# A two-block network on one core: gates ahead of gMLP's mixing, another order of routing, and an extra expert slot of 64 places

## The chip, the core and the metric

The kernel runs on one core of one Trainium2 chip. The metric is the device time of one execution in microseconds (us), with all inputs and outputs in device memory. A core has TensorE (PE, matrix products into PSUM), VectorE (DVE), ScalarE (ACT) and GpSimd (POOL) on the on-chip memory, SyncE (SP), which here issues most transfers, and 16 transfer engines that all queues share. POOL issues the indirect transfers (gather and scatter of rows) and those that add to what lies in memory.

## What is computed

512 positions of width 1024 pass through two residual blocks, all in float32. The reference, cut to what matters here:

```python
x = first_block(x, ...)          # SSD and RWKV mixers, then a gated feed-forward net
h = rms_norm(x, g1) * (1 + sc1) + sh1
ys = gmlp(h), gla(h), sparse_attention(h)                 # (512, 512) each
gate = sigmoid(h @ w_gates + b)                           # (512, 3, 1024)
merged = sum over n of gate[:, n] * (ys[n] @ w_branch[n]) # 24 tiles of 128 columns
x = x + gt1 * (merged @ w_out)
h2 = rms_norm(x, g2) * (1 + sc2) + sh2
grp = argmax(softmax(h2 @ w_group + b_group))             # 1 of 4 groups of 4 experts
e1, e2 = top 2 of the router's logits in that group
x = x + gt2 * sum over e in (e1, e2) of weight_e * (silu(h2 @ Wg[e]) * (h2 @ Wu[e])) @ Wd[e]
```

gMLP mixes positions inside chunks of 128: `y = u * (w_s @ layer_norm(v) + b_s)`, a lower triangular `w_s` for each of four groups of columns. An expert has 1024 x 256 weights for Wg and Wu and 256 x 1024 for Wd.

## The kernel before

**Products.** A float32 product is made of three faster ones: `split` (L186, L187) and the weight loads (L155, L156 and, for the experts, L1307, L1308) make of a tile a rounded part `hi` on ACT and the remainder `lo` on DVE; then hi x hi, lo x hi and hi x lo are added in PSUM (L170 to L172). Weights come in pieces of 512 KB, 128 x 1024, by SP. The trace shows such a split product with PE rows of three lines; a product of plain f32 operands stands as two rows.

**The start.** Seventeen products of zeros (L278) run until the first operands are there. SP loads `vec` (L136), then the eight blocks of x (L284); ACT loads the first raw weights (L283).

**Branches and gates.** `ev_v` (L1066 to L1074) evaluates gMLP's `v` with gelu on ACT and normalises it on DVE. The mixing products (L1078) need all of `v`, then L1079 and L1080 make `u`, and `merge(0, u)` (L986) splits it into `yh` and `yl`. `merge(n)` runs over eight column tiles d: a gate product (24 instructions, `gemm` with `win2`, tanh on ACT at L991), then the branch product (12, `wbr`), then one or two operations on DVE (L993 to L996). Up to the routing a scheduler sets each engine's order, by costs and due times; it mixes the sparse attention (L1092 to L1105) with the merge of gMLP. Two tiles `th` hold gates.

**Routing.** The second half of `w_out` and the routing have their order written out. For each block of 128 positions tb: eight products (`product`, L1312), with the block before turned (`turned`, transposes L1321), its logits (`logits` L1325, `added` L1328 to L1331) in between; then `x2half` (L1279 to L1281) adds the residual and squares on ACT; `inverse` (L1333 and the Newton steps L228 to L233) makes 1/rms; `scaled` (L1336) and `rows_out` (L1340 to L1344) write h2's rows to the DRAM buffer `d_h2`. For blocks 0 and 1 `d_h2` is filled with the shift sh2 beforehand and POOL adds the rows to it (L1341); for blocks 2 and 3 DVE adds the shift (L1343) and SP writes (L1344). Then DVE finds group, experts and each row's place in its expert's list (L1365 to L1408), and POOL gathers the first 128 rows (L1467).

**Experts.** 17 slots of 128 places: 16 experts, and a slot 16 for the first expert whose list is longer than 128; its number is read from a register, and a branch covers further overflow. A slot e: rows are gathered (L1467), transposed (L1473) and split; four up pieces (L1484 to L1486, 24 instructions); silu on ACT (L1488), the product on DVE (L1489); transposes (L1493); two down pieces (L1503 to L1506, of which L1506 is plain f32 and has no split); DVE scales (L1507), and POOL scatters the rows to `out`, adding (L1508). The loop (L1541) computes up(e+1) between the parts of down(e). Five of the six pieces of a slot are split on ACT and DVE. SP issues the weight loads in the order of `todo`, as slots of a ring of some 22 tiles come free; only the first ten are asked for ahead of the first gather (`hold`). `further` (L1425) works out on DVE, in five steps, which experts overflow; `extra` (L1443) looks up the rows of the overflow in one piece at e = 11. In the order rows below, numbers behind names such as `gv_8091` are buffers.

## Time and profile before

| quantity | value |
|---|---|
| three runs | 1485.41, 1489.78, 1494.95 us; median 1489.78 us |
| profiled execution | 1490.69 us; span 1488.9 us, granted clock 0.979 |
| PE busy | 1423.3 us, 96% of the span |
| DVE busy | 1028.4 us, 69% |
| ACT busy | 642.4 us, 43% |
| POOL busy | 94.9 us, 6% |
| from HBM / to HBM | 208.06 / 27.03 MB |
| expert stage | PE resumes at 1299.43 us, last scatter issued at 1478.26 us |

The span runs from the first to the last instruction; the profiled execution has 1.8 us around it. Busy shares are means over stages with different limits. Where PE is busy almost all the time, what counts is which wait interrupts it, at which clock it runs, and what lies behind its last product.

### The profile page before, as it was taken

The numbers are of one execution on the slowest core, as the hardware profiler recorded it, in microseconds if no ns is written. First come the engines' busy times: TensorE is split into PE (matmuls) and PEld (weight loads), VectorE is DVE, ScalarE is ACT, GpSimd is POOL, SyncE is SP. The second block draws the span as 40 slices with busy tenths as digits, with TensorE's granted clock in tenths as the row PEclk, the third lists the DMA queues.
The fourth block names the chain that finished last, engine by engine and source line by source line (L and its number), as shares of the span: only waits on it lengthen the run. The fifth ranks groups of instructions, "written<-read, shape, count | busy, mean of one in ns | idle before, by whom it ended". The sixth has DMA issues, their size and how long they took to land. (4 is left out here: it accounts for less than half of the span.)

```text
span 1488.9 us, 22888 instructions
## 1 busy us (share of the span) xinstructions
PE 1423.3 (96%) x8863; PEld 1107.0 (74%) x8863; DVE 1028.4 (69%) x1948; ACT 642.4 (43%) x1045; POOL 94.9 (6%) x114
## 2 busy tenths in 40 slices
PE   9999998999999999999999989999899999599996
PEld 5777877677777787778777777777678887377774
DVE  6788977578777767544749867654544344789995
ACT  6554374234443443223443324463622333266663
POOL 0121000000000000000001000000000000123321
PEclk9999998999999999999999999999999999799999
DMA  5347234143556535553424211222044234499992
GB/s 215 134 154 251 85 112 133 66 142 124 167 177 212 183 115 188 172 170 114 146 99 140 92 57 50 64 95 80 23 167 138 92 127 165 142 391 362 331 342 58
DMA packets 78885, 226.16 MB, mean 152 GB/s; under 512 B 19571, under 2 KB 20211, under 8 KB 78771
## 3 DMA queue, kind: packets, MB, share of 16 engines
q1 hardware_dynamic: 68626, 201.79, 39.0%
q0 software_dynamic: 8992, 19.71, 4.8%
q10 hardware_dynamic: 1152, 3.15, 0.5%
q8 instruction: 71, 1.16, 0.3%
q14 instruction: 44, 0.35, 0.1%
HBM read 208.06 MB, written 27.03 MB: 158 GB/s over the span
## 5 line engine op out<-in xcount | busy, mean ns | idle before, releaser
L155 ACT ACTIVATE hi<-raw 128x1024 fp32r<-128x1024 f32 (+1 forms) x181 | 181.1, 1001 | 395.6 <-PE g L171 255.2
L156 DVE TENSOR_TENSOR lo<-raw,hi 128x1024 fp32r<-128x1024 f32 (+1 forms) x181 | 208.1, 1150 | 203.5 <-ACT hi L155 202.9
L172 PE MATMUL g<-bh,lo 128*128 128x512 f32 x376 | 152.4, 405 | 2.6 <-DVE lo L156 2.4
L170 PE MATMUL g<-bh,hi 128*128 128x512 f32 x376 | 152.1, 405 | 0.0
L171 PE MATMUL g<-bl,hi 128*128 128x512 f32 x376 | 150.3, 400 | 0.0
L170 PE MATMUL g<-hh,hi 128*128 128x512 f32 x336 | 133.1, 396 | 0.0
L172 PE MATMUL g<-hh,lo 128*128 128x512 f32 x336 | 132.7, 395 | 0.2 <-DVE lo L156 0.2
L171 PE MATMUL g<-hl,hi 128*128 128x512 f32 x336 | 132.6, 395 | 0.0
L172 PEld LDWEIGHTS g<-bh,lo 128*128 128x128 f32 x376 | 71.5, 190 | 22.6 <-DVE lo L156 4.1
L170 PEld LDWEIGHTS g<-bh,hi 128*128 128x128 f32 x376 | 71.7, 191 | 19.3 <-issue 2.4
L171 PEld LDWEIGHTS g<-bl,hi 128*128 128x128 f32 x376 | 71.4, 190 | 16.2 <-issue 0.2
L170 PE MATMUL g<-xh,hi 128*128 128x512 f32 x192 | 76.8, 400 | 0.0
L170 PEld LDWEIGHTS g<-hh,hi 128*128 128x128 f32 x336 | 63.3, 188 | 17.7 <-ACT hi L155 2.5
L172 PE MATMUL g<-xh,lo 128*128 128x512 f32 x192 | 76.4, 398 | 0.0
L171 PE MATMUL g<-xl,hi 128*128 128x512 f32 x192 | 76.2, 397 | 0.0
L172 PEld LDWEIGHTS g<-hh,lo 128*128 128x128 f32 x336 | 63.3, 188 | 15.5 <-DVE lo L156 0.6
L171 PEld LDWEIGHTS g<-hl,hi 128*128 128x128 f32 x336 | 63.3, 189 | 14.6
L885 DVE SCALAR_TENSOR_TENSOR acc<-raw,ca,acc 128x1024 f32<-128x1024 f32 x42 | 53.8, 1282 | 28.7 <-DMA raw<-in_wmod 28.4
L914 DVE SCALAR_TENSOR_TENSOR c<-g,vec,c 128x511 f32<-128x511 f32 x88 | 65.6, 745 | 1.1
L777 PE MATMUL g<-hi,fh 128*128 128x512 f32 x136 | 53.9, 396 | 0.0
L779 PE MATMUL g<-lo,fh 128*128 128x512 f32 x136 | 53.7, 395 | 0.0
L778 PE MATMUL g<-hi,fl 128*128 128x512 f32 x136 | 53.7, 395 | 0.0
(705 smaller groups left out, 3200.7 us busy)
## 6 DMA issues: line engine op xcount, KB each, us to landing
raw<-in_wexp SPq DMA_DIRECT2D x89, 512.0 KB, 13.2
raw<-in_win SPq DMA_DIRECT2D x72, 512.0 KB, 3.5
raw<-in_wmod SPq DMA_DIRECT2D x48, 512.0 KB, 4.1
raw<-in_wup SPq DMA_DIRECT2D x44, 512.0 KB, 4.3
raw<-in_wdn SPq DMA_DIRECT2D x22, 512.0 KB, 3.9
raw<-in_wout SPq DMA_DIRECT2D x16, 512.0 KB, 4.8
ws<-in_wexp SPq DMA_DIRECT2D x13, 512.0 KB, 14.3
raw<-in_wA SPq DMA_DIRECT2D x12, 512.0 KB, 3.9
```

The costliest lines, as they stand in the source:

```text
L155: S.activation(hi[:,:f],raw[:,:f],AF.Copy)
L156: V.tensor_tensor(lo[:,:f],raw[:,:f],hi.bitcast(F32)[:,:f],op=OP.subtract)
L170: PE.matmul(ps,hi[:,sl],xh[k],start=(k==0),stop=False)
L171: PE.matmul(ps,hi[:,sl],xl[k],start=False,stop=False)
L172: PE.matmul(ps,lo[:,sl],xh[k],start=False,stop=(k==n-1))
L777: PE.matmul(ps,xh[k][:,sl],w[kk][0],start=(k==0),stop=False)
L778: PE.matmul(ps,xl[k][:,sl],w[kk][0],start=False,stop=False)
L779: PE.matmul(ps,xh[k][:,sl],w[kk][1],start=False,stop=(k==2*n-1))
L885: else: V.scalar_tensor_tensor(acc,raw,ca[:,k:k+1],acc,op0=OP.mult,op1=OP.add)
L914: for k in (1,2): V.scalar_tensor_tensor(c[:,k:],ps[:,:512-k],Vc(f'fw{2-k}',i),c[:,k:],op0=OP.mult,op1=OP.add)
```

## The change

Six things are done at once.

- Start: `vec` is loaded on ACT's queue, x's first block is asked for first on SP, and two of the seventeen zero products go.
- Gates: `gate(n, d)` makes one gate ahead of its use; three are made before gMLP's mixing, and `merge` keeps three ahead. Four tiles `th` instead of two.
- Routing: all four blocks' rows are added by POOL to a `d_h2` that is filled with the shift for all 512 rows, so the tile of the shift goes. `rows_out(tb-1)` and `added(tb-1)` stand before the last three products of block tb; the last block is scaled before its inverse and multiplied by it on ACT.
- Clock: 13 products whose result nobody reads (`keep_going`) stand between the places' products and the first slot, and five before the last down product.
- Look-up: `extra` becomes `extra_steps`, four pieces at e = 7 to 10; `further` starts one slot earlier, and a further overflow test is added (a list of more than 192 rows, or a second overflow, takes the branch).
- Extra slot: it holds 64 places and runs between experts 14 and 15. Its products are plain f32 on unsplit weights, each in two halves of 64 columns of the array (`up64`, `down64`), so none of its six pieces is split; expert 15 comes last.

Places where the order moves, engine by engine.

PE around the last of gMLP's mixing (`m<-wst`, L1078 before, L1086 now; `g<-bh`, `g<-bl` are gate products, `m<-kn` the attention's first product). Before:

```order
L170 MATMUL g<-bh,hi 128x512
L171 MATMUL g<-bl,hi 128x512
L172 MATMUL g<-bh,lo 128x512
L1078 MATMUL m<-wst,gv_8127 128x128 x4
L1078 MATMUL m<-wst,gv_8145 128x128 x4
L1092 MATMUL m<-kn_7624,yq_7068 128x128
L170 MATMUL g<-yh,hi 128x512
```

Now, from the fourth mixing product on; behind the dots stand gate products alone, then the other twelve mixing products:

```order
L1086 MATMUL m<-wst,gv_8107 128x128
L172 MATMUL g<-bh,lo 128x512
L170 MATMUL g<-bh,hi 128x512
L171 MATMUL g<-bl,hi 128x512
...
L172 MATMUL g<-bh,lo 128x512
L1086 MATMUL m<-wst,gv_8125 128x128
L1086 MATMUL m<-wst,gv_8143 128x128
...
L1086 MATMUL m<-wst,gv_8143 128x128
L1100 MATMUL m<-kn_7622,yq_7066 128x128
L170 MATMUL g<-yh,hi 128x512
```

Of the 72 instructions of the first three gates, 71 stand ahead of the last twelve mixing products; before, 32 gate instructions stood ahead of the last eight.

DVE from block 3's residual to the first operation of the routing (`L1365` before, `L1372` now). Before:

```order
L1280 TENSOR_TENSOR x1t<-x1t,g_11690 128x512
L1343 SCALAR_TENSOR_TENSOR h_11643<-h_11643,nv,modr 128x1024
L1333 TENSOR_SCALAR nv<-ssq 128x1
...
L1336 TENSOR_TENSOR h_11705<-x1t,modr 128x1024
L1329 TENSOR_REDUCE l_11723<-m 128x20
L1330 TENSOR_TENSOR lg<-lg,l_11723 128x20
L1331 SCALAR_TENSOR_TENSOR lg<-lg,nv,rbias 128x20
L1343 SCALAR_TENSOR_TENSOR h_11705<-h_11705,nv,modr 128x1024
L1365 TENSOR_REDUCE mx_11738<-lg 128x20
```

Now:

```order
L1348 SCALAR_TENSOR_TENSOR h_11675<-x1t,nv,modr 128x1024
L1337 TENSOR_REDUCE l_11680<-m 128x20
L1338 TENSOR_TENSOR lg<-lg,l_11680 128x20
L1339 SCALAR_TENSOR_TENSOR lg<-lg,nv,rbias 128x20
L1287 TENSOR_TENSOR g_11687<-g,modr 128x512
L1288 TENSOR_TENSOR x1t<-x1t,g_11687 128x512
L1344 TENSOR_TENSOR h_11692<-x1t,modr 128x1024
L1341 TENSOR_SCALAR nv<-ssq 128x1
...
L1337 TENSOR_REDUCE l_11720<-m 128x20
L1339 SCALAR_TENSOR_TENSOR lg<-lg,nv,rbias 128x20
L1372 TENSOR_REDUCE mx_11733<-lg 128x20
```

Block 2's rows (L1348) stand ahead of block 3's residual instead of behind it; block 3's scaling stands ahead of its inverse, and no pass over its rows is left before L1372.

PE in the extra slot, which before was a slot like the others. Now (`L1533` transposes, `L1540` up, `L1553` down, `L1512` and `L1492` transposes of the neighbours):

```order
L1533 MATMUL m<-cst,xg 128x64 x8
L1522 MATMUL g<-hi,ah 128x512
...
L1525 MATMUL g<-raw,af 128x512
L1540 MATMUL g<-raw,xf 64x256 x8
L1512 MATMUL m<-cst,a 128x128 x2
L1540 MATMUL g<-raw,xf 64x256 x8
L1492 MATMUL m<-cst,xg 128x128 x8
...
L1547 MATMUL m<-cst,a_13445 128x64 x2
...
L1553 MATMUL g<-raw,af_13494 64x512 x4
```

Sixteen up and four down products stand in place of 24 and eight, and expert 15's products follow between and behind them.

The diff, changed lines only:

```diff
@@ -133,7 +133,7 @@
-    vec=cp.tile([128,A['vec'].shape[1]],F32,name='vec'); nc.sync.dma_start(vec,A['vec'])
+    vec=cp.tile([128,A['vec'].shape[1]],F32,name='vec'); nc.scalar.dma_start(vec,A['vec'])
@@ -275,13 +275,14 @@
-        for _ in range(17): PE.matmul(zp,zb[:,:128],zb,start=True,stop=True)
+        for _ in range(15): PE.matmul(zp,zb[:,:128],zb,start=True,stop=True)
...
+        nc.sync.dma_start(xt[0],A['xT'][0])
...
-        for k in range(8): nc.sync.dma_start(xt[k],A['xT'][k])
+        for k in range(1,8): nc.sync.dma_start(xt[k],A['xT'][k])
@@ -966,7 +967,8 @@
-    mpool=pool('mp',bufs=2,stack=ph2)
+    GA=3
+    mpool=pool('mp',bufs=GA+1,stack=ph2)
@@ -981,14 +983,19 @@
+    gates={}
+    def gate(n,d):
+        ps=gemm(w2b(23+8*n+d),hh,hl)
+        gates[n,d]=th=mpool.tile([128,512],F32,name='th',tag='th'); S.activation(th,ps,AF.Tanh,bias=bgh[:,8*n+d:8*n+d+1],scale=0.5)
...
-            ps=gemm(w2b(23+8*n+d),hh,hl)
-            th=mpool.tile([128,512],F32,name='th',tag='th'); S.activation(th,ps,AF.Tanh,bias=bgh[:,8*n+d:8*n+d+1],scale=0.5)
+            for d2 in range(d,min(8,d+GA)):
+                if (n,d2) not in gates: gate(n,d2)
+            th=gates[n,d]
@@ -1035,7 +1042,7 @@
-    with tc.issue_after(oh_.ins): nc.sync.dma_start(d_h2[0:256,:],bass.AP(tensor=d_mod.tensor,offset=d_mod.offset+3072,ap=[[0,256],[1,1024]]))
+    with tc.issue_after(oh_.ins): nc.sync.dma_start(d_h2,bass.AP(tensor=d_mod.tensor,offset=d_mod.offset+3072,ap=[[0,512],[1,1024]]))
@@ -1073,6 +1080,7 @@
+    for d in range(GA): gate(0,d)
@@ -1228,7 +1236,7 @@
-    slots=[(rawm,'raw')]*NR+[(wr,'raw')]*4+[('pe',f'modr{i}') for i in (0,2,1)]+[(res_pool,f'res{i}') for i in range(4)]+[('AS',0),('AS',1),('AS',2),('AS',3),('pe2','rx0')]
+    slots=[(rawm,'raw')]*NR+[(wr,'raw')]*4+[('pe',f'modr{i}') for i in (1,0,2)]+[(res_pool,f'res{i}') for i in range(4)]+[('AS',0),('AS',1),('AS',2),('AS',3),('pe2','rx0')]
@@ -1240,7 +1248,7 @@
-    for e in range(1,16): todo+=wx(e,range(4))+wx(e-1,(4,5))
+    for e in range(1,15): todo+=wx(e,range(4))+wx(e-1,(4,5))
@@ -1257,10 +1265,10 @@
-    for i in range(4):
+    for i in (0,2,3):
...
-    gt1r,sh2r,a2r,gt2r=modr
+    gt1r,a2r,gt2r=modr
@@ -1309,9 +1317,9 @@
-    def product(tb,ps,p):
+    def product(tb,ps,p,kks=(0,1)):
...
-        for kk in range(2):
+        for kk in kks:
@@ -1336,26 +1344,25 @@
-        if tb<2:
+        if tb<3:
...
-            G.dma_start(d_h2[tb*128:tb*128+128,:],h,accum_op=OP.add)
...
-            h=blk[tb]['h']; V.scalar_tensor_tensor(h,h,v,sh2r,op0=OP.mult,op1=OP.add)
-            nc.sync.dma_start(d_h2[tb*128:tb*128+128,:],h)
+            h=blk[tb]['h']; S.activation(h,h,AF.Copy,scale=v)
+        G.dma_start(d_h2[tb*128:tb*128+128,:],h,accum_op=OP.add)
...
-        product(tb,ps,3)
-        if tb: added(tb-1)
+        product(tb,ps,3,(0,))
+        if tb: rows_out(tb-1); added(tb-1)
+        product(tb,ps,3,(1,))
...
-        if tb: rows_out(tb-1)
+        if tb==3: scaled(tb)
...
-        if tb>=2: scaled(tb)
-    turned(3); logits(3); added(3); rows_out(3)
+    turned(3); logits(3); rows_out(3); added(3)
@@ -1403,6 +1410,10 @@
+    def keep_going(n):
+        w=pt()
+        for _ in range(n): PE.matmul(w,trib[:,:128],Ak[:,0:4,:].rearrange('p i s -> p (i s)'),start=True,stop=True)
+    keep_going(13)
@@ -1439,32 +1450,40 @@
-        V.tensor_copy(ei[:,0:7],EQ[:,0,0:7]); V.tensor_copy(ei[:,7:8],pos[:,47:48])
-    def extra(j,ps,s):
+        mc=pe_.tile([128,1],F32,name='mc'); V.tensor_reduce(mc,cnt,axis=AX,op=OP.max)
+        V.scalar_tensor_tensor(mc,mc,192.5,pos[:,47:48],op0=OP.is_gt,op1=OP.add)
+        V.tensor_copy(ei[:,0:7],EQ[:,0,0:7]); V.tensor_copy(ei[:,7:8],mc)
+    def extra_steps(j,ps,s,upper=False):
...
-        V.tensor_scalar(cc,cc,EQ[:,1,j:j+1],None,op0=OP.subtract)
+        V.tensor_scalar(cc,cc,EQ[:,1,j:j+1],64.0 if upper else 0.0,op0=OP.subtract,op1=OP.subtract)
+        yield
...
+        yield
...
-        return onehot(cc),lambda tb:tb_[:,tb,:],ps,s
+        yield
+        O=onehot(cc)
+        if upper: V.memset(O[:,:,64:],0.0)
+        yield O,lambda tb:tb_[:,tb,:],ps,s
+    def extra(*a,**k): return list(extra_steps(*a,**k))[-1]
...
-    for s_ in range(1,17): pieces+=[(s_,p) for p in range(4)]+[(s_-1,4),(s_-1,5)]
-    pieces[-6:]=[(16,0),(16,1),(15,4),(15,5),(16,2),(16,3),(16,4),(16,5)]
+    for s_ in range(1,15): pieces+=[(s_,p) for p in range(4)]+[(s_-1,4),(s_-1,5)]
+    pieces+=[(16,p) for p in range(4)]+[(14,4),(14,5),(15,0),(15,1),(16,4),(16,5)]+[(15,p) for p in range(2,6)]
...
-            s_,p=pieces[len(done)]; done.append(wnext(p==5 or (s_<NW and p<4)))
+            s_,p=pieces[len(done)]; done.append(wnext(p==5 or s_==16 or (s_<NW and p<4)))
...
-    def gather(ix):
+    def gather(ix,n=128):
...
-        G.indirect_dma_start(out=xg,out_offset=None,in_=d_h2,in_offset=bass.IndirectOffsetOnAxis(ap=ix,axis=0),bounds_check=511,oob_is_err=False)
+        G.indirect_dma_start(out=xg[:n],out_offset=None,in_=d_h2,in_offset=bass.IndirectOffsetOnAxis(ap=ix,axis=0),bounds_check=511,oob_is_err=False)
@@ -1507,6 +1526,34 @@
+    def rows64(xg):
+        xf=pe2.tile([128,8,64],F32,name='xf',tag='xgl',bufs=1)
+        for hf in range(2):
+            ps=pt((128,4,64))
+            for kk in range(4): PE.transpose(ps[:,kk,:],xg[:64,(4*hf+kk)*128:(4*hf+kk)*128+128],ident[:64,:64])
+            S.activation(xf[:,4*hf:4*hf+4,:],ps,AF.Copy)
+        return xf
+    h64=lambda e: slice(64*e,64*e+64)
+    def up64(ps,xf,p,raw):
+        for kk in range(2):
+            k=2*p+kk
+            for e in range(2): PE.matmul(ps[h64(e),:256],xf[:,k],raw[:,kk*512+256*e:kk*512+256*e+256],start=(k==0),stop=(k==7))
+    def end64(ps,wcol):
+        u=sq_pool.tile([64,256],F32,name='u64',tag='sq',bufs=3); V.tensor_scalar(u,ps[64:,:256],wcol[:64],None,op0=OP.mult)
+        a=sq_pool.tile([64,256],F32,name='a64',tag='sq',bufs=3); S.activation(a,ps[:64,:256],AF.Silu)
+        V.tensor_tensor(a,a,u,op=OP.mult); return a
+    def act64(a):
+        pT=pt((128,2,64))
+        for f in range(2): PE.transpose(pT[:,f,:],a[:,f*128:f*128+128],ident[:64,:64])
+        af=pe2.tile([128,2,64],F32,name='af64',tag='afx',bufs=1); S.activation(af,pT,AF.Copy)
+        return af
+    def down64(af,raws,ix):
+        y=pe2.tile([128,1024],F32,name='ye',tag='ye',bufs=3); ps=psum()
+        for f in range(2):
+            for e in range(2): PE.matmul(ps[h64(e)],af[:,f],raws[f][:,512*e:512*e+512],start=(f==0),stop=(f==1))
+        for e in range(2): V.tensor_tensor(y[:64,512*e:512*e+512],ps[h64(e)],gt2r[h64(e),512*e:512*e+512],op=OP.mult)
+        G.indirect_dma_start(out=out,out_offset=bass.IndirectOffsetOnAxis(ap=ix,axis=0),in_=y[:64],in_offset=None,
+                             bounds_check=511,oob_is_err=False,compute_op=OP.add)
@@ -1538,36 +1585,49 @@
-    for e in range(17):
+    for e in range(14):
...
-        if e<13: xgs.append(gather(idx[:,e+4:e+5]))
-        if e==3: fur=further()
-        if 3<=e<8: next(fur,None)
-        if e==11: xps=pm.tile([128,17,8],F32,name='m',tag='m'); O=extra(0,xps,16)
-        if e==8:
+        if e<11: xgs.append(gather(idx[:,e+4:e+5]))
+        else: xgs.append([lambda:gather(idx[:64,16:17],64),lambda:gather(idx[:,15:16]),lambda:None][e-11]())
+        if e==2: fur=further()
+        if 2<=e<7: next(fur,None)
+        if e==7: xst=extra_steps(0,None,16)
+        if 7<=e<10: next(xst)
+        if e==10: xps=pm.tile([128,17,8],F32,name='m',tag='m'); o_=next(xst); O=(*o_[:2],xps,16)
+        if e==7:
...
-            w0=[(A['wexp'][bass.ds(e0,1),p].rearrange('o p f -> (o p) f'),p==5) for p in range(6)]
-            todo+=w0[:2]+wx(15,(4,5))+w0[2:]
-        if e<16: ps=psum(); up_piece(ps,xin,0,piece(e+1,0))
+            w0=[(A['wexp'][bass.ds(e0,1),p].rearrange('o p f -> (o p) f'),True) for p in range(6)]
+            todo+=w0[:4]+wx(14,(4,5))+wx(15,(0,1))+w0[4:]+wx(15,range(2,6))
+        ps=psum(); up_piece(ps,xin,0,piece(e+1,0))
...
-        if e<16:
-            for p in range(1,4):
-                if e==15 and p==2: down(aa,piece(e,4),piece(e,5),idx[:,e:e+1])
-                up_piece(ps,xin,p,piece(e+1,p))
-            a=up_end(ps,wcl[:,e+1:e+2])
+        for p in range(1,4): up_piece(ps,xin,p,piece(e+1,p))
+        a=up_end(ps,wcl[:,e+1:e+2])
...
-        if e<15: xin=rows_in(xgs[e+2],e+2)
-        if e!=15: down(aa,piece(e,4),piece(e,5),idx[:,e:e+1])
+        xin=rows_in(xgs[e+2],e+2) if e<13 else rows64(xgs[15])
+        down(aa,piece(e,4),piece(e,5),idx[:,e:e+1])
...
+    ps=psum()
+    for p in range(2): up64(ps,xin,p,piece(16,p))
+    aa=act_in(a)
+    for p in range(2,4): up64(ps,xin,p,piece(16,p))
+    a=end64(ps,wcl[:,16:17])
+    xin=rows_in(xgs[16],15)
+    down(aa,piece(14,4),piece(14,5),idx[:,14:15])
+    ps=psum(); up_piece(ps,xin,0,piece(15,0)); af=act64(a)
+    up_piece(ps,xin,1,piece(15,1))
+    down64(af,(piece(16,4),piece(16,5)),idx[:64,16:17])
+    for p in range(2,4): up_piece(ps,xin,p,piece(15,p))
+    a=up_end(ps,wcl[:,15:16]); keep_going(5)
+    down(act_in(a),piece(15,4),piece(15,5),idx[:,15:16])
...
-    nx=nc.values_load(ei[0:1,7:8],min_val=0,max_val=7)
+    nx=nc.values_load(ei[0:1,7:8],min_val=0,max_val=8)
...
-        for j in range(1,7): placed(*extra(j,xps,j))
-        infos(xps,1,7,wc2,ix2)
-        for j in range(1,7):
+        for j in range(7): placed(*extra(j,xps,j,upper=j==0))
+        infos(xps,0,7,wc2,ix2)
+        for j in range(7):
```

## Rows read from the trace of the kernel before

**Rows 1.** Waits of PE over the whole span: total us, times, longest us.

```profile
PE m L1473 <- DMA xg<-d_h,idx: 5.8, 1, 5.8
PE g L172 <- DVE lo L156: 2.6, 4, 1.8
PE g L1486 <- DVE ws L1308: 1.9, 1, 1.9
```

**Rows 2.** Windows: from:to, length; busy us of each engine, granted clock, DMA share, GB/s.

```profile
888.00:898.00 10.00, 5.95 (x23) 5.00 (x24) 8.63 (x18) 4.04 (x7) 0.00 (x0) 0.68 0.19 72
1300.00:1340.00 40.00, 38.86 (x177) 29.41 (x176) 34.62 (x56) 27.42 (x40) 9.39 (x7) 0.94 1.02 384
1340.00:1380.00 40.00, 40.00 (x180) 29.99 (x178) 39.47 (x56) 27.35 (x42) 15.06 (x8) 1.00 1.01 360
1380.00:1420.00 40.00, 40.00 (x180) 30.19 (x179) 36.86 (x50) 27.25 (x41) 11.40 (x9) 1.00 0.99 341
1420.00:1460.00 40.00, 38.14 (x171) 28.93 (x170) 36.56 (x54) 23.76 (x37) 8.97 (x5) 0.96 0.88 304
```

**Rows 3.** Timeline of the start: start us, duration, engine, line, operation, idle before.

```profile
0.76 0.40 SPq L136 DMA_DIRECT2D vec<-in_vec  x1
6.43 0.72 ACT L189 ACTIVATE xh<-x,vec 128x512 fp32r<-128x512 f32 x1 [2.29 <-DMA x<-in_xT]
```

**Rows 4.** Timeline, PE at the last gMLP mixing.

```profile
890.45 1.16 PE L1078 MATMUL m<-wst,gv 128*128 128x128 f32 x8 [2.77 <-DVE gv L1074]
892.74 2.08 PE L1078 MATMUL m<-wst,gv 128*128 128x128 f32 x8 [1.14 <-DVE gv L1074]
895.71 0.80 PE L170 MATMUL g<-yh,hi 128*128 128x512 f32 x1 [0.46 <-ACT yh L186]
```

**Rows 5.** Timeline, DVE between the last product and the first routing operation.

```profile
1286.12 1.28 DVE L1343 SCALAR_TENSOR_TENSOR h<-h,nv,modr 128x1024 f32<-128x1024 f32 x1
1287.32 0.23 DVE L1365 TENSOR_REDUCE mx<-lg 128x20 f32<-128x80 f32 x1
```

**Rows 6.** Timeline, POOL's first row gather and PE's resumption.

```profile
1294.96 1.19 POOL L1467 DMA_INDIRECT xg<-d_h,idx  x1 [17.45 <-DVE idx L1408]
1299.43 1.94 PE L1473 MATMUL m<-cst,xg 128*128 128x128 f32 x8 [5.84 <-DMA xg<-d_h,idx]
```

**Rows 7.** One line, the two accumulating row writes.

```profile
DMA to landing us min/median/max: 5.0/5.1/5.2
```

**Rows 8.** Timeline, PE: f32 products of 64 columns, then of the whole array.

```profile
215.65 0.39 PE L600 MATMUL g<-ring,Sin 128*64 128x128 f32 x4
215.87 0.39 PE L598 MATMUL g<-ring 128*64 128x128 f32 x4
...
934.28 1.05 PE L1104 MATMUL m<-pT,dv 128*128 128x128 f32 x8
935.09 0.48 PE L171 MATMUL g<-yl,hi 128*128 128x512 f32 x1
```

**Rows 9.** Timeline, down products of three expert slots, and DVE's look-up between.

```profile
1417.37 0.79 PE L1503 MATMUL g<-ws,ah 128*128 128x512 f32 x1
...
1421.50 0.23 DVE L1445 TENSOR_SCALAR eq<-cst,EQ 128x16 f32<-128x16 f32 x1
...
1424.35 0.68 DVE L1411 TENSOR_TENSOR O<-cst,xcc 128x512 bf16<-128x512 f32 x1
...
1440.90 0.80 PE L1503 MATMUL g<-hi,ah 128*128 128x512 f32 x1
...
1450.71 0.79 PE L1503 MATMUL g<-hi,ah 128*128 128x512 f32 x1
```

**Rows 10.** One line, the loads of the expert weights.

```profile
DMA to landing us min/median/max: 3.6/13.2/18.0
```

**Rows 11.** Chain that ended last: start us, us, what.

```profile
1471.65 5.84 DMA out<-ye,idx
```

**Rows 12.** One line, the scatters of the expert rows.

```profile
DMA to landing us min/median/max: 3.9/9.0/10.6
```

## The prediction, on record before the change was timed

> **What bounds the kernel now.** I read the waits of TensorE (PE) first, because PE is busy for 96% of the span: a change can only gain what PE idles, what it does at half clock, what it need not do, and what lies behind its last product. The waits [rows 1] name two places that the diff touches, 5.8 us for the first gathered rows and 1.9 us in an expert slot, and in the timeline gMLP's mixing [rows 4]. Then the windows [rows 2], to be read in two columns. The granted clock, against 1.00, tells where PE runs at the lower of its two levels (1.2 instead of 2.4 GHz): 0.68 at 888 to 898, 0.94 at 1300 to 1340, 0.96 at 1420 to 1460. The DMA share tells how full the transfer engines are during the experts: 1.02, 1.01, 0.99, then 0.88. PE is busy for all 40 us of two of these windows, yet the transfers are full too, so what PE gains there may not be kept. Last the chain that ended last [rows 11]: behind the last product the end is a row of scatters, each waiting for the one before.
>
> **Start.** SP's load of `vec` takes 0.40 us of issue ahead of x, and ACT's first split waits for x [rows 3]. On ACT's queue it delays the raw blocks instead. Bounds: 0 and -0.4; I take **-0.3**, since x is the one named as the releaser.
>
> **Gates ahead of the mixing.** PE idles 2.77, 1.14 and 0.46 us here [rows 4], 4.37 in all. The clock of 0.68 means 64% of 10 us at half speed, 6.4 us; 1.6 of these are the last two gaps, so some 4.8 us of work cost 2.4 too much. The ceiling is 6.8 us. In the new order 71 gate products stand ahead of the last mixing products where there were 32; 39 at 0.222 us (180 in the 40 us of a full window [rows 2]) are 8.7 us, more than gap and slow clock together. PE does no less work; it pays because those 8.7 us go missing later, where they cover nothing that the rows show waiting. The price is on DVE, busy 8.63 of these 10 us [rows 2]: it makes two more low halves before the split of `u`, and ACT's `yh` still follows the mixing. For those waits I keep 0.8, taken from the 0.46 and 1.14 that PE waits today; if the split comes late by the whole 2.77 the gain is 3.5. **-6.0**, between -3.5 and -6.8. The later gates only trade places: every product keeps its weights, its conversions and its load on SP, which are asked for in the new order.
>
> **Routing.** DVE's two passes by line 1343, of which [rows 5] show the second, 1.28 us, are on the path: the first, alike, stands ahead of the last inverse, the second delays routing's first operation to 1287.32. The change puts the first one before the block's last products end and leaves the second to ACT, behind which nothing waits but POOL's write. So 2 x 1.28 go, and the third block's logits move ahead of the last three products, 0.7 us, of which I count 0.5; the last logits still pass ACT and PE and may come when DVE has long been free, for which I take 0.7 back (no row shows when). **-2.4**, between -1.3 (one pass) and -3.1. The new danger is the write: accumulating writes took 5.0 to 5.2 us to land [rows 7]. If POOL issues the last no earlier than DVE finished it before, 1286.12 + 1.28, it lands at 1292.6; the gather, now at 1294.96 [rows 6] less 2.4, starts at 1292.6 as well. So it costs nothing until it is late, then one for one. The prefilled rows add 1 MB long before, in stretches where the transfers have room (share 0.19 at 888 to 898).
>
> **Clock at the first slot.** PE waits 5.84 us for the rows and resumes at 1299.43 [rows 6]. A clock of 0.94 over 40 us is 4.8 us at half speed, 2.4 us lost. Thirteen 512-column products at half clock (twice 0.222 us) are 5.8 us and just fit into the wait. They buy the clock, but then the first pieces' conversions on ACT and DVE decide: **-1.6**, between 0 and -2.4.
>
> **Look-up in four steps.** From the down product of one slot to the next takes 9.81 us (1440.90 to 1450.71), and the two slots with the look-up take 23.53 [rows 9]: 3.91 too much, of which 1.9 is PE's wait for DVE [rows 1] and the rest clock (0.96). On DVE it runs from 1421.50 to 1425.03, 3.5 us with one short break [rows 9]. In four steps, four slots to one slot earlier, it falls into 1382 to 1412. At 1380 to 1420 DVE is busy 36.86 of 40 us, so 0.77 per slot is free for 0.9 per slot. **-3.4**, between -2 and -3.9. DVE at 39.47 of 40 one window earlier says how thin that cover is.
>
> **Extra slot of 64 places.** Today a slot: 9.81 us. In f32 a product stands as two records. With 64-column outputs the next four records follow after 0.22 us; with the whole array eight take 0.81 [rows 8], so 0.055 against 0.101 each: the two column halves run together. The new slot's 16 products of 256 columns are 32 records of twice the length, 3.5 us; its 4 of 512 columns 8 records of four times, 1.7; ten smaller transposes at 0.055 add 0.6: 5.8. **-4.0**; one after the other it would be 6.5 + 3.2 + 0.6 = 10.3, +0.5, the other bound. The Trainium skill (TensorEngine Tiling (Array Packing), "Key Properties") says that a change of tiling mode drains TensorE, which speaks against a slot that goes in and out of it. As an estimate, the 0.17 us by which a group of [rows 8] outlasts the next one's start, at six changes, is 1.0, and the sum would be -3.0; no row here shows such a drain.
>
> **What the transfers take back.** Clock, look-up and slot give 9.0 us after the weights have begun to flow (routing's 2.4 moves the flow too). The transfers have 12% of 40 us, 4.8, to spare in one window, none before [rows 2]; gather and scatter of 64 rows instead of 128 save 0.5 MB, 1.4 us at 341 to 360 GB/s. So between 0 and 2.8 us of the gain must wait for weights that are asked for 13.2 us ahead [rows 10]: **+1.3**, the middle. Expert 15's pieces, now last, are where it shows.
>
> **Tail.** The last scatter was the extra slot's, which holds the fewest rows; I take the shortest for it, 3.9 us [rows 12]. It becomes expert 15's, which took 5.84 [rows 11]: **+2.0**. The five fillers ahead of the last transposes cost 0.1 at most beside a wait that is there anyway.
>
> **Sum.** -0.3 - 6.0 - 2.4 - 1.6 - 3.4 - 4.0 + 1.3 + 2.0 = -14.4. The profiled execution took 1490.69 us (span 1488.9, 1.8 around it), 0.9 above the median: 1476.3 for such an execution, **1475** for the median.
>
> **Rivals.**
> - *Nothing taken back*: no late weights (1.3), no leftover at gates, look-up (0.8, 0.5) and clock (0.8): 1472. For it: DVE and transfers have some slack wherever the gain falls. Against: three of four windows at 0.99 or more.
> - *The halves do not run together*, so that the slot does not do what it is cut for: +4.5, 1480. Against: 0.055 per record; for: those records move 128 columns, these 256 and 512.
> - *The transfers keep their old pace*: the whole 9.0 is lost instead of 1.3, 1483. For it: shares of 0.99 to 1.02; against: 0.88, and PE, not the queue, set the two long slots.
> - *Slower than before*: in the merges the branch products now follow gates of which three are ahead, and DVE's low halves come late. PE waited for low halves 4 times, 2.6 us [rows 1]. If each of the 24 branch products waited such 0.65 us, it would be 15.6: 1491; at the longest, 1.8, 43 us: 1518. It decides from 0.6 us per product for slower at all, from 1.25 for slower by over 1%. Against: only four such waits in all the gemms now.
>
> **Numbers.** Forecast 0.50 (its own range 1469 to 1481), nothing taken back 0.15, halves 0.15, transfers 0.14, slower 0.04, the rest 0.02. A run of this kernel tells 1% from no change: 14.9 us, 1474.9. The forecast lies on that line, so half of it counts as faster: 0.25 + 0.15 + the rest of 0.02, 0.42. Within 1%: 0.55. Slower by over 1%: 0.03, the long form of the last rival. The range 1467 to 1484 takes in the first three rivals and the bounds of the gates and the slot.
>
> **What would show it.** Right: no PE gap over 0.5 us and a clock near 1.00 at 885 to 900; routing's first reduction about 2.4 us sooner against the last product; no half clock behind the first gather; no wait for DVE in the look-up's slots; the extra slot at 5 to 7 us between its neighbours; the last scatter near 5.8. Wrong: PE waits for conversions whose weights have just landed, in expert 15 above all; a gather that waits for POOL's last accumulating write; new waits for low halves between gates and branch products; a mixing that waits as long as before, only later.

## The result, and the profile after

The changed kernel takes **1480.63 us** (median of 13 runs, 1475.24 to 1487.36) against 1489.78 us for the kernel before (13 runs beside them): ratio 0.9936, 95% interval 0.9919 to 0.9952, so 9.2 us or 0.6% faster. The forecast was 14.4 us. The profiled execution took 1484.45 us, span 1482.7 us, granted clock 0.979.

To see where the time went I cut both traces at the same events, each the start of an instruction, and compare the stretches between them (us; "again" is a second profile of the change, its text unchanged, span 1482.2). The first stretch begins with the span:

| from the event before to | before | after | again |
|---|---|---|---|
| second block's `hn`, first product | 718.31 | 720.92 | 718.37 |
| first product of the linear attention's own gate | 266.30 | 259.39 | 259.01 |
| its first score product | 47.35 | 46.72 | 46.72 |
| its last | 33.11 | 35.19 | 35.07 |
| routing's first transpose | 184.51 | 184.40 | 185.03 |
| routing's first reduction (`mx`) | 37.74 | 35.12 | 35.11 |
| PE's first transpose of gathered rows | 12.11 | 12.17 | 12.23 |
| third slot's transposes (so: two slots) | 17.85 | 18.22 | 18.22 |
| last down product | 159.13 | 152.44 | 153.48 |
| end | 12.49 | 18.12 | 18.96 |

Gates give 7.5 us (rows two and three; 7.9 in the second profile), but 2.1 and 2.0 of it go again in row four, and PE's clock went with them:

```profile
1031.96:1065.07 33.11, 27.23 (x917) 20.14 (x916) 27.01 (x70) 19.71 (x56) 0.00 (x0) 0.95 0.05 14
```

```profile
1027.03:1062.22 35.19, 28.99 (x917) 21.68 (x916) 28.02 (x71) 20.70 (x57) 0.00 (x0) 0.86 0.09 32
```

These are row four's windows (columns as in [rows 2]), before and after: the same 917 products, the granted clock 0.95 and 0.86. Routing gives 2.6 us. PE reaches its last product 6.7 us sooner after the third slot began (5.6 in the second profile), but 5.6 to 6.5 us are lost behind that product. From the third slot to the end it is 171.6 us before, 170.6 and 172.4 after. The 2.6 us in the first stretch is no work of the change: from 100 to 120 us the granted clock was 0.83 in this profile, 0.91 in the second and 1.00 before, and a run below whose start is that of the kernel before (four pieces ahead) takes 721.40 us here.

Windows of the changed kernel, columns as in [rows 2]:

```profile
886.00:896.00 10.00, 10.00 (x49) 8.27 (x48) 9.86 (x30) 2.82 (x4) 0.00 (x0) 1.00 0.23 79
896.00:906.00 10.00, 9.28 (x54) 7.95 (x53) 5.59 (x12) 4.59 (x8) 0.00 (x0) 1.00 0.23 79
1290.00:1330.00 40.00, 36.42 (x164) 26.64 (x163) 33.26 (x58) 26.62 (x38) 9.89 (x9) 0.94 0.96 358
1330.00:1370.00 40.00, 40.00 (x181) 30.34 (x180) 39.69 (x59) 26.62 (x41) 13.43 (x8) 1.00 1.02 370
1370.00:1410.00 40.00, 40.00 (x185) 30.17 (x184) 39.42 (x54) 26.59 (x41) 13.60 (x8) 1.00 0.97 336
1410.00:1450.00 40.00, 40.00 (x201) 28.67 (x199) 31.93 (x45) 23.40 (x39) 10.14 (x6) 1.00 0.97 334
1430.00:1450.00 20.00, 20.00 (x107) 13.43 (x106) 13.20 (x18) 9.80 (x19) 3.16 (x2) 1.00 0.93 331
```

The clock at the mixing is 1.00 where it was 0.68, and the 40 us from 1410 run at 1.00 without a gap where those from 1420 had 0.96 and 38.14 busy [rows 2]. Only 1290 to 1330 still shows 0.94.

The timeline of the changed kernel, PE at the mixing and the extra slot, ACT before it, then POOL and DVE at the end:

```profile
899.91 2.84 PE L1086 MATMUL m<-wst,gv 128*128 128x128 f32 x24
903.70 0.50 PE L170 MATMUL g<-yh,hi 128*128 128x512 f32 x1 [0.72 <-ACT yh L186]
...
1443.29 1.95 PE L1540 MATMUL g<-raw,xf 128*64 128x256 f32 x16
1445.17 0.44 PE L1512 MATMUL m<-cst,a 128*128 128x128 f32 x2
1445.54 1.95 PE L1540 MATMUL g<-raw,xf 128*64 128x256 f32 x16
1454.81 1.94 PE L1553 MATMUL g<-raw,af 128*64 128x512 f32 x8
...
1443.89 1.06 ACT L1315 ACTIVATE ws<-raw 128x1024 fp32r<-128x1024 f32 x1 [3.40 <-DMA raw<-in_wexp]
...
1458.57 1.54 POOL L1527 DMA_INDIRECT out<-ye,idx  x1 [6.46 <-DVE ws L1316]
1465.01 1.43 POOL L1555 DMA_INDIRECT out<-ye,idx  x1 [4.90 <-DVE ye L1526]
1465.20 0.69 DVE L1526 TENSOR_TENSOR ye<-g,modr 128x512 f32<-128x512 f32 x1 [0.87 <-PE g L1525]
1470.19 1.55 POOL L1527 DMA_INDIRECT out<-ye,idx  x1 [3.74 <-DMA out<-ye,idx]
```

Read the last three together. Expert 15's result is complete at 1465.20 + 0.69 = 1465.89, but its scatter is issued at 1470.19, 4.3 us late: all scatters add to `out`, each waits for the one before, and the extra slot's went off at 1465.01. Before, the last result was complete at 1477.73 and its scatter issued at 1478.26, 0.5 us later. The releaser at 1465.01 reads `DVE ye`, yet that scatter too started just behind its predecessor, which landed at 1464.26 in the chain of the changed kernel (start us, us, what):

```profile
1410.92 9.29 DMA out<-ye,idx
...
1422.02 9.15 DMA out<-ye,idx
1431.97 9.40 DMA out<-ye,idx
1442.16 7.64 DMA out<-ye,idx
1450.55 7.24 DMA out<-ye,idx
1458.57 5.69 DMA out<-ye,idx
1465.01 4.42 DMA out<-ye,idx
```

Here is the bound that [rows 11] showed only the end of: from 1410.92 on the end is set by scatters. Most start 0.8 us behind the landing of the one before; they are some 9 us long, and shorter towards the end. PE is busy for every one of the 40 us to 1450 and does not stand in this chain.

### The profile page after: what moved, and what is told of

The parts are those of the page before. It is cut to its first block, busy times and chain, and to the rows that moved or that the text cites. A ratio compares the mean times of both kernels' runs of the same rounds, so it can differ in the third digit from the quotient of the medians.

```text
span 1482.7 us, 22891 instructions
## 1 busy us (share of the span) xinstructions
PE 1422.2 (96%) x8883; PEld 1103.1 (74%) x8885; DVE 1019.0 (69%) x1941; ACT 635.6 (43%) x1038; POOL 97.4 (7%) x116
## 4 chain that ended last, share of the span: by engine, by line
PE 77%; DVE 10%; DMA 5%; issue 3%; ACT 3%; SPq 0%; POOL 0%; POOLq 0%; ACTq 0%; DVEq 0%
PE g L172 14%; PE g L170 13%; PE g L171 13%; PE g L778 4%; PE g L779 4%; PE g L780 4%; DMA out<-ye,idx 4%; PE g L982 2%; PE g L983 2%; PE g L984 2%; PE g L1504 1%; PE m L213 1%; PE g L1505 1%; PE g L1503 1%; DVE sc L1033 1%
```

## The experiments

The theory is that the PE time that look-up and extra slot save is real, but that the row of scatters sets the end, at a pace that the stream of weights gives it. There are two rivals: PE waits for weights that land late; or the new place of the extra slot alone costs the tail. For each run "two slots" is the stretch of that name in the table above (17.85 before), "stage" the time from the third slot's transposes to the end (171.6 before; 170.6 and 172.4 for the change), and the lag is that of the last scatter behind its data (0.5 before, 4.3 and 4.6 for the change).

| run | ratio to before (95%) | median us | two slots | stage | lag |
|---|---|---|---|---|---|
| gates not ahead | 0.9971 (0.9952 to 0.9989) | 1487.41 | 18.21 | 170.5 | 3.1 |
| no fillers | 0.9914 (0.9893 to 0.9935) | 1481.49 | 17.45 | 169.9 | 1.6 |
| look-up in one step | 0.9932 (0.9914 to 0.9951) | 1482.48 | 18.23 | 170.3 | 1.7 |
| extra slot of 128 | 0.9906 (0.9889 to 0.9923) | 1479.34 | 17.44 | 169.8 | 1.3 |
| no scatter of the extra slot | 0.9915 (0.9888 to 0.9942) | 1480.23 | 16.67 | 169.1 | 0.3 |
| fewer loads | 0.9895 (0.9869 to 0.9921) | 1476.69 | 16.69 | 166.7 | 0.3 |
| five pieces ahead | 0.9900 (0.9876 to 0.9923) | 1477.33 | 16.67 | 167.5 | 0.9 |
| before, four ahead | 1.0010 (0.9994 to 1.0026) | 1491.71 | 17.42 | 170.3 | 0.8 |
| five ahead, extra slot last | 0.9883 (0.9866 to 0.9899) | 1475.61 | 18.26 | 166.5 | 1.2 |
| that, rows first | 0.9887 (0.9868 to 0.9907) | 1474.26 | 16.27 | 166.4 | 0.9 |
| that, no 13 fillers | 0.9904 (0.9883 to 0.9926) | 1477.25 | 17.60 | 166.9 | 0.6 |
| the change again | 0.9924 (0.9900 to 0.9948) | 1481.59 | 18.22 | 172.4 | 4.6 |

**Gates not ahead.**

```diff
-    GA=3
+    GA=1
...
-    for d in range(GA): gate(0,d)
```

> The change without its gates ahead (each gate is made right before its use, none ahead of the mixing). By the prediction's term PE idles and runs at half clock at the mixing again: 6.0 us more than the change. By the traces of before and after the change wins 7.5 us between the attention's start and GLA's first products, and gives 2.6 back up to the next stage: 4.9 more than the change at the end of the merges, 1485.5, 0.997. Rival: the gates covered GLA's waits before, and all is given back: 0 to 2 more. The scatters' lag at the end stays 4 us in each case.

The timeline of this run, PE:

```profile
891.00 1.16 PE L1085 MATMUL m<-wst,gv 128*128 128x128 f32 x8 [2.77 <-DVE gv L1081]
893.30 2.07 PE L1085 MATMUL m<-wst,gv 128*128 128x128 f32 x8 [1.14 <-DVE gv L1081]
896.26 0.79 PE L170 MATMUL g<-yh,hi 128*128 128x512 f32 x1 [0.46 <-ACT yh L186]
```

The three waits of [rows 4] are back to the hundredth, and the second stretch of the table is 267.05 us instead of 259.39. By the medians this one part carries more than half of what the whole change gains. Row four is 33.37 us here, at a granted clock of 0.95. In the three profiles without gates ahead (this one, before, and before with four pieces ahead) it takes 33.1 to 33.4 us; with gates ahead it takes 34.8 to 35.4 in seven of eleven (clock 0.86 to 0.88) and 32.6 to 33.1 in four (0.95). So what row four takes back is seen only with the gates ahead, but not each time, and no run shows what decides it.

**No fillers.**

```diff
-        for _ in range(n): PE.matmul(w,trib[:,:128],Ak[:,0:4,:].rearrange('p i s -> p (i s)'),start=True,stop=True)
+        for _ in range(0): PE.matmul(w,trib[:,:128],Ak[:,0:4,:].rearrange('p i s -> p (i s)'),start=True,stop=True)
```

> The change without its 18 filler products. By the prediction's term PE starts the first slot at half clock again: 1.6 us more than the change. By the traces slot 0 took 9.49 us before and 7.8 in every run with the fillers, so 1.7 comes back in that slot; slot 1 then waits 1.7 us for ACT and DVE with the fillers (0.85 and 0.83) and 1.1 without (0.82 and 0.31), so the two slots together lose 1.1 to 1.4. At the end, where the last scatter waits 4.3 us for the one before (theory A), 1.1 to 1.4 us later on PE costs only what starts the row of scatters later: the same 1.1 to 1.4, since that row runs without a break from slot 1 on. Rival B (PE alone sets the end): the same 1.1 to 1.4. Expected ratio 0.9944 in both.

The run came out at 0.9914 instead of the expected 0.9944, no slower than the change. The first slot takes 9.0 us instead of 7.78, the second 8.45 instead of 10.44: both together are 0.8 us shorter without fillers than in the changed kernel's profile. The timeline of the changed kernel shows why, PE and ACT:

```profile
1303.58 0.51 PE L1503 MATMUL g<-hi,xgh 128*128 128x512 f32 x1 [0.85 <-ACT xgh L186]
1304.91 0.79 PE L1504 MATMUL g<-hi,xgl 128*128 128x512 f32 x1 [0.83 <-DVE xgl L187]
...
1301.36 1.28 ACT L1507 ACT_TABLE_LOAD   x1
1302.65 0.38 ACT L1507 ACTIVATE a<-g 128x256 f32<-128x256 f32 x1
1302.93 1.08 ACT L186 ACTIVATE xgh<-m 128x512 fp32r<-128x512 f32 x2
```

The second slot's rows wait on ACT behind the silu of the first and its table load, PE stands twice, and half clock follows, from 1304.92 to 1308.33. In three runs with the fillers (no scatter, fewer loads, five ahead) that second stretch did not come, and the two slots took 16.67 to 16.69 us; in the run with 128 places it came in the first slot instead.

**Look-up in one step.**

```diff
-        if e==7: xst=extra_steps(0,None,16)
-        if 7<=e<10: next(xst)
-        if e==10: xps=pm.tile([128,17,8],F32,name='m',tag='m'); o_=next(xst); O=(*o_[:2],xps,16)
+        if e==10: xps=pm.tile([128,17,8],F32,name='m',tag='m'); O=extra(0,xps,16)
```

> The change with the look-up in one piece at e = 10. Rival B (PE sets the end): PE's wait and the half clock come back, 3.4 to 3.9 us more than the change, 1484.3, 0.996. Theory A (the row of scatters sets the end, 4.3 us behind PE at the last slot): the row runs 4 to 6 us behind PE from slot 10 on, so the lost PE time is taken from that lag: slots after the look-up come 3.9 us later, the lag at the last scatter falls from 4.3 to 0.4, and the end moves by less than 1 us: 1480.6 to 1481.5, 0.9936 to 0.9942.

The timeline of this run, PE:

```profile
1408.02 0.50 PE L1505 MATMUL g<-lo,xgh 128*128 128x512 f32 x1 [1.88 <-DVE lo L1316]
```

The wait of [rows 1] is back, and the slot takes 12.05 us, as 12.04 before. The slot behind it keeps its 9.79 us, where the kernel before had 11.50: the half clock did not come back, so this run undoes 2.2 of the 4.0 us. After the third slot PE's last down product comes 2.1 us later than in the changed kernel (1.1 later than in its second profile), the end does not: 170.3 against 170.6, and the lag fell from 4.3 to 1.7. PE time there is not on the path of the end.

**Extra slot of 128 places,** last, split and scheduled as before, all else as changed.

```diff
-    for e in range(1,15): todo+=wx(e,range(4))+wx(e-1,(4,5))
+    for e in range(1,16): todo+=wx(e,range(4))+wx(e-1,(4,5))
...
-    for e in range(14):
+    for e in range(17):
...
+        if e==16: keep_going(5)
+        if e!=15: down(aa,piece(e,4),piece(e,5),idx[:,e:e+1])
```

> The change with the extra slot as before: 128 places, split weights, last. By the prediction's terms, 4.0 us on PE and 2.0 in the tail the other way: 2.0 more than the change. Theory A: PE ends some 2.5 to 4 us later than in the change, but the row of scatters, which was 4.3 us behind, no longer waits, and its last link is the short one (3.5 to 3.9 instead of 5.8): the end comes -2 to +1 us of the change's, so the 64 places alone bring nothing: 1478.6 to 1481.6. The last scatter starts under 1.5 us after its data.

PE's last down product is 3.7 us later than in the changed kernel (156.11 against 152.44), and the stage is no longer: 169.8. So the slot of 64, in its new place, saves PE 2.6 to 3.7 us (by the two profiles of the change) and the end nothing.

**No scatter of the extra slot.** The one accumulating transfer of `down64` goes.

```diff
-        G.indirect_dma_start(out=out,out_offset=bass.IndirectOffsetOnAxis(ap=ix,axis=0),in_=y[:64],in_offset=None,
-                             bounds_check=511,oob_is_err=False,compute_op=OP.add)
```

> The change without the scatter of the extra slot's rows (its few rows are left out of the output; the slot is computed all the same). Theory A, the row of scatters sets the end: each starts 0.8 us after the one before has landed, and in the change the last one starts 4.3 us after its data are ready. One link of about 5.2 us less (1465.0 to 1470.2) lets expert 15's scatter start 0.3 to 0.5 us after its data: the end comes 3.8 to 4.0 us sooner than in the change, about 1476.7, 0.991 of before. Rival B, the end follows PE and the weights: the last product and the end stay where they are, 1480.6, 0.9936.

The timeline of this run, ACT, PE, DVE and POOL:

```profile
1443.95 1.06 ACT L1315 ACTIVATE ws<-raw 128x1024 fp32r<-128x1024 f32 x1 [5.11 <-DMA raw<-in_wexp]
1451.43 0.49 PE L1503 MATMUL g<-ws,xgh 128*128 128x512 f32 x1 [1.46 <-ACT xgh L186]
...
1465.76 0.69 DVE L1526 TENSOR_TENSOR ye<-g,modr 128x512 f32<-128x512 f32 x1 [0.87 <-PE g L1525]
1466.73 1.55 POOL L1527 DMA_INDIRECT out<-ye,idx  x1 [7.74 <-DVE ye L1526]
```

The lag is gone, 0.28 us, yet the stage gains only 1.5 to 3.3 us of the 3.8 to 4.0 expected: with one scatter fewer, late weights are next. ACT waits 5.11 us for a piece that has just landed, and PE 1.46 behind it; PE's last down product comes 2.2 us later than in the changed kernel. The two bounds lie close behind each other, and scatters and weights move through the same full transfers (share 0.94 from 1430 to 1450).

**Fewer loads.** The second down pieces of experts 4 to 14 are not loaded; expert 3's stands for them, so 11 of 102 pieces.

```diff
+    same=lambda e,p: p==5 and 4<=e<=14
...
-    wx=lambda e,ps_: [(A['wexp'][e,p],p==5 or e<NW) for p in ps_]
+    wx=lambda e,ps_: [(A['wexp'][e,p],p==5 or e<NW) for p in ps_ if not same(e,p)]
...
```

> The change with the sixth weight piece of experts 4 to 14 not loaded (expert 3's piece is used again, so these experts' outputs are others): 11 of 102 pieces, about 14 us of transfer time, less, spread over the expert stage. If the length of a scatter (9 to 10 us while weights flow, 5.8 behind them) is load on the transfer engines, the scatters of these slots take 7 to 8 us, the lag behind their data goes under 1 us before the last slots, and the end comes about 4 us sooner than in the change (1476.5). If it is a fixed latency, they keep 9 to 10 us and the lag stays 4 us (1480.6). Rival B (PE sets the end): PE's periods stay 9.77 us and the end 1480.6 in either case.

**Five pieces ahead.** Same loads, five of them asked for before the routing, when the transfers idle (share 0.36 at 1235 to 1245 and 0.00 at 1245 to 1255 of the changed kernel).

```diff
+    for _ in range(5): wfetch(*todo.pop(0))
     late=[None]
```

> The change with five more weight pieces (2.5 MB) asked for ahead of the routing, when the transfers have almost nothing to do (share 0.36 and 0.00 at 1235 to 1255), instead of behind the first gather. Theory A with load: the stream of weights ends about 6.5 us sooner, the last two or three scatters meet fewer weights and take 6 to 7 instead of 7 to 9 us, the lag at the last one goes from 4.3 to about 1: 3 us sooner than in the change, 1477.5, 0.9915. Rival B: PE does not wait for weights in the slots, so nothing changes (1480.6), or it is worse by the conversions of pieces that come in another order.

The window from 1410 to 1430 of the changed kernel, and the same of the run with fewer loads:

```profile
1410.00:1430.00 20.00, 20.00 (x96) 15.24 (x94) 18.73 (x27) 13.60 (x21) 6.99 (x4) 1.00 1.01 336
```

```profile
1410.00:1430.00 20.00, 20.00 (x92) 15.21 (x91) 18.66 (x27) 13.83 (x21) 6.59 (x4) 1.00 0.99 332
```

The window behind it, fewer loads first, then five ahead (the changed kernel's stands above, share 0.93):

```profile
1430.00:1450.00 20.00, 20.00 (x104) 13.23 (x104) 12.94 (x18) 8.13 (x15) 4.71 (x3) 1.00 0.24 61
```

```profile
1430.00:1450.00 20.00, 20.00 (x106) 13.44 (x105) 13.16 (x19) 7.89 (x16) 3.24 (x2) 1.00 0.58 184
```

And the last scatters in the chain of the run with five ahead:

```profile
1426.86 9.24 DMA out<-ye,idx
1436.89 7.61 DMA out<-ye,idx
1445.25 4.83 DMA out<-ye,idx
1450.87 6.70 DMA out<-ye,idx
1458.32 3.51 DMA out<-ye,idx
```

Both runs win 3 to 6 us in the stage, and all of it behind PE: its last product comes 152.39 and 152.44 us after the third slot began, as in the change (152.44). But the first did not win it in the way I had expected: while weights flow a scatter stays at 9 to 11 us with a ninth of the pieces gone. The stream was not thinner for it, share 0.99 against 1.01 up to 1430; it ended sooner. That is what changes in both runs. With five ahead the share is 0.58 where it was 0.93, the scatters shrink sooner (expert 13's, the same rows, takes 4.83 us where it took 7.24), and the row has caught up with PE at the last: lag 0.89. In time five ahead has 0.9900 and the change 0.9936 and 0.9924, with intervals that overlap; the stage of the profiles is the clearer sign.

**Before, four ahead.** The same edit, four pieces, in the kernel before.

> The kernel before with four weight pieces asked for ahead of the routing and nothing else changed. If the change moved the bound (before, the row of scatters and PE end together: the last scatter starts 0.5 us after its data and ACT never waits for weights), four pieces sooner bring the kernel before at most 0.5 to 1 us: ratio 0.9995. If transfers already set the end before, they bring the 3 us that five brought to the change: 0.998.

Expert 14's scatter on POOL, in the kernel before with its data on DVE, then in this run:

```profile
1463.46 1.28 DVE L1507 TENSOR_TENSOR ye<-g,modr 128x512 f32<-128x512 f32 x2
1465.02 1.54 POOL L1508 DMA_INDIRECT out<-ye,idx  x1 [7.49 <-DVE ye L1507]
```

```profile
1465.55 1.54 POOL L1509 DMA_INDIRECT out<-ye,idx  x1 [5.06 <-DVE ye L1508]
```

Nothing in time: 1.0010, at best 0.9994, though the stage is 1.3 us shorter in its profile. In both this scatter starts 0.3 us after its data: the row, which had been up to 4.8 us behind, has caught up with PE and its two long slots, and the last two scatters follow 1.4 us or less behind their data. So earlier transfers are worth nothing that shows; in the changed kernel, where the row stays 2.3 us or more behind its data from 1350 on, five pieces are worth 3 us or more of the stage. That is the bound having moved from PE to the transfers, shown by one edit on either side, though with four pieces here and five there.

**Five ahead, extra slot last.** With `up64` and `down64` as in the change, after expert 15, so the shortest scatter is again the last.

```diff
-    for e in range(14):
+    for e in range(15):
...
     for p in range(2): up64(ps,xin,p,piece(16,p))
     aa=act_in(a)
+    down(aa,piece(15,4),piece(15,5),idx[:,15:16])
     for p in range(2,4): up64(ps,xin,p,piece(16,p))
...
+    a=end64(ps,wcl[:,16:17]); keep_going(5)
+    af=act64(a)
     down64(af,(piece(16,4),piece(16,5)),idx[:64,16:17])
...
```

> Meant to beat both: five weight pieces asked for ahead of the routing, and the extra slot of 64 places last, so that the row of scatters ends with its shortest link (3.5 instead of 5.7 us), with expert 15's down product ahead of the extra slot's second half. Theory A: the last scatter starts under 1 us after its data, and the end comes 1.5 to 2.5 us sooner than with the five pieces alone: 1475.3, 0.9885. Rival: expert 15's scatter (5.8 us and 0.8) is not over when the extra slot's rows are ready, and what the short link wins is waited for before it: 1477.3, 0.990.

1475.61 us. Against five ahead alone the intervals overlap, so the slot's place by itself is worth 1 us in the stage (166.5 against 167.5) and not more that I can show.

**Rows first, and rows first without the 13 fillers.** On top of that, the second slot's rows are split before the first slot's silu; then the fillers before the first slot go.

```diff
+    xin=rows_in(xgs[1],1); xgs.append(gather(idx[:,3:4]))
     wpc=pe_.tile([128,48],F32,name='wpc'); V.tensor_copy(wpc,wps[:,:48])
...
     a=up_end(ps,wcl[:,0:1])
-    xin=rows_in(xgs[1],1); xgs.append(gather(idx[:,3:4]))
```

> Five pieces ahead, the extra slot last, and the second slot's rows split ahead of the first slot's silu. In every run with fillers PE waits 0.85 us for ACT and 0.83 for DVE at the second slot, because ACT takes silu and DVE three small operations and the product first. If that order is the cause, the first two slots take 15.5 to 16.2 us instead of 16.7 or 18.2, without the second half-clock stretch, and the whole 1474.4, 0.9875 or less. Rival: the first slot's own chain (silu, product, transposes) waits instead, and nothing is gained: 0.9883.

> The same without the thirteen fillers ahead of the first slot. If they buy the clock for that slot and the second slot no longer gives it back, this one takes 9.0 us in the first slot instead of 7.8 and is 1.2 us slower; if ACT and DVE set the pace of the first two slots in any case, the two together take the same and so does the whole.

The timeline of the run with rows first, PE's waits in the second slot, and the last scatter on POOL:

```profile
1298.58 0.50 PE L1504 MATMUL g<-hi,xgh 128*128 128x512 f32 x1 [0.25 <-ACT xgh L186]
1299.37 0.50 PE L1505 MATMUL g<-hi,xgl 128*128 128x512 f32 x1 [0.29 <-DVE xgl L187]
...
1461.39 1.44 POOL L1556 DMA_INDIRECT out<-ye,idx  x1 [5.13 <-DVE ye L1555]
```

The waits shrink from 0.85 and 0.83 us to 0.25 and 0.29, the two slots take 16.27 us; without the fillers 17.60, so here the fillers are worth 1.3. The version with rows first, 1474.26 us, and the one it stands on, 1475.61 us, are the fastest of the case, ahead of both kernels: 0.9887 and 0.9883 of the kernel before, where the change had 0.9936 and 0.9924. Which of the two is faster is not settled.

**The change again,** its text unchanged.

> The change itself once more (a space in one line), beside the next three on the same chip. 0.9936 as before if its ratio holds from chip to chip. What it settles: in its first profile PE fell to half clock in the second slot and the first two slots took 18.2 us, in three of its variants 16.7. If that is chance, this profile may show either; the third slot to the end should take 170.6 us again, and the last scatter start 4 us after its data.

The timeline of this run, ACT, DVE and POOL:

```profile
1442.05 1.06 ACT L1315 ACTIVATE ws<-raw 128x1024 fp32r<-128x1024 f32 x1 [3.92 <-DMA raw<-in_wexp]
...
1463.87 0.69 DVE L1526 TENSOR_TENSOR ye<-g,modr 128x512 f32<-128x512 f32 x1 [0.87 <-PE g L1525]
1469.14 1.55 POOL L1527 DMA_INDIRECT out<-ye,idx  x1 [3.89 <-DMA out<-ye,idx]
```

Lag 4.6 us, the late weight on ACT and the half clock in the second slot are all there again; they belong to the change and not to one execution. Here PE did wait behind ACT and DVE in expert 15's slot, 0.27 and 0.23 us, and its last product came 153.49 us after the third slot began instead of 152.44; the last scatter still started 4.6 us behind its data.

## Why the prediction came out as it did

- **Start** (-0.3): the first split of x begins at 6.08 us instead of 6.43 [rows 3], -0.35. It now waits for `vec` and the table load behind it, no longer for x.
- **Gates** (-6.0): -7.5 up to the linear attention's scores, 0.72 us of waiting left where I had kept 0.8, and +2.1 in the scores, at a lower clock. Up to the routing (rows two to five) that is -5.6, and -5.4 in the second profile. Undoing them costs the run about as much: 0.9971 against 0.9936 and 0.9924. The size is right; that the gates' 8.7 us go missing where they cover nothing is not shown, since row four lost its 2 us only in profiles with the gates ahead. The late low halves of the slower rival did not come: PE's waits for them grew from 2.6 to 4.2 us over the whole span, where 15.6 were needed.
- **Routing** (-2.4): -2.6. The accumulating write was issued at 1282.34 and took 5.1 us; the gather at 1289.32 did not wait for it.
- **Clock at the first slot** (-1.6): -1.7 in the first slot, as forecast, but in both profiles of the change it is given back in the second by a half-clock stretch of its own. The two slots give +0.4 there and -1.2 where that stretch does not come. I had looked at the first slot alone.
- **Look-up** (-3.4): 23.53 us for two slots became 19.54 for the same two, 4.0 less on PE. Right on PE.
- **Extra slot** (-4.0): the rest of PE's 6.7 us (5.6 in the second profile), -2.7 (-1.7); undoing it gives 2.6 to 3.7. Its products take 3.90 and 1.94 us for the 3.5 and 1.7 worked out, so the halves do run together: one after the other it would have been 6.5 and 3.2. The products take 0.6 us more than worked out, less than the 1.0 that the prediction estimated from [rows 8] for six changes of mode. The Trainium skill (TensorEngine Tiling (Array Packing), "Key Properties") states that a change of tiling mode drains TensorE; the 0.6 us do not contradict it, but no run takes them apart.
- **What transfers take back (+1.3) and tail (+2.0): the step that failed.** Together +3.3 forecast; behind the last product +5.6 and +6.5. The first term was written for the wrong waiter. I let PE wait for weights, and PE did not (40.00 us of 40 to 1450); ACT did, 3.40 us, without holding PE up; in the second profile PE waited 0.5 us in all. The second term priced expert 15's scatter by its own length, as if it could start when its data is there. The length was right: of the 5.6 us, 1.9 is the longer last scatter (from its issue to the end 12.5 us, 10.6 before). But it starts when the extra slot's has landed, 4.3 us after its data instead of 0.5, and for these 3.8 us the sum had no term. The sign was in [rows 12], with [rows 11]: at 9.0 us for the median scatter and 0.8 between two, the row advances every 9.8 us, just as a slot of PE did (9.81, [rows 9]). PE could not get faster there without leaving the row behind. The 0.5 MB that I let the smaller slot save were not all there either: the extra slot's scatter moved only 0.01 MB in the kernel before.

So look-up and extra slot, 6.7 and 5.6 us on PE, moved the end by -1.0 us in one profile and +0.8 in the other. Everything forecast for the experts (clock, look-up, slot, transfers, tail) came to -5.7; with the first two slots it measured -0.7 and +1.2. That the time still lies inside the range of 1467 to 1484 is owed to start, gates and routing, which came out as forecast, and to the range's width; the forecast of the experts was not right. The rival of the transfers that keep their pace named the resource, not the mechanism. The mechanism is shown by three kinds of edit: PE time taken away again costs the end nothing (one step, 128 places), earlier or fewer transfers bring 3 to 6 us in the stage at the same PE time, and earlier transfers bring nothing to the kernel before. Of the rivals, PE's late weights are seen, but as the next bound (no scatter), and the extra slot's place is worth 1 us. What stays open is how long a scatter takes beside a thinner stream of weights: no run made one.

## What to carry to other kernels

A row of transfers that wait for each other has a pace of its own, duration plus the gap between two; compare it with the period of the engine that feeds it before counting anything saved on that engine as time. When two resources run at the same period, as here, speeding up one only shifts the lag to the end, and the edit that pays is the one on the other (here five loads asked for while the transfers idle). The fillers that kept the clock up here paid until the next wait; look one stage further for what stands there.

## What the runs showed of the hardware that was not expected

- An accumulating scatter of 128 places took 7.6 to 10.7 us beside the stream of weights, and 8.8 to 11 with a ninth of the pieces left out, at the same transfer share. Once the stream had ended it took 4.5 to 6.8, and the extra slot's 3.1 to 4.6.
- The places were mostly empty towards the end, and the time fell far less than the bytes. In the kernel before expert 15's scatter moved 0.15 MB, some 36 rows of 4 KB, in 5.84 us, and the extra slot's 0.01 MB, some three rows, in 3.87.
- Two waits of PE of 0.85 and 0.83 us were followed by 3.4 us at half clock in both profiles of the change, and 0.25 and 0.29 by none; other runs of the same stretch escaped it, for a reason that the traces do not show. The two waits were the same there within 0.01 us.
